# A hybrid encoder layer on one core: side work in the projection phase, first weight loads, dummy matmuls and Newton buffers rearranged

## The chip, the cores and the metric

The kernel runs on one core of a Trainium2 chip. The core has TensorE (PE, matrix products into PSUM), VectorE (DVE), ScalarE (ACT), GpSimd (POOL) and SyncE (SP), and 16 DMA engines that move data between device memory and the on-chip SBUF. Each engine works through its own instruction queue in order, and waits on semaphores for the others. The metric is the device time of one execution in microseconds (us); lower is better.

## The reference

Two inputs, a prompt of 512 tokens and a sample of 2048, go through one encoder layer with shared weights. All 1024-wide matrix products are float32.

```python
def encoder_layer(x, pre_g, post_g, w_in, ...):
    h = rms_norm(x, pre_g)
    z = h @ w_in                       # q k v, gates, u_b, c_val, c_glu, merge gates
    ...
    y_a = neighbourhood_attention(heads(q), heads(k), heads(v), rpb) * jax.nn.silu(gate_a)
    y_b = fourier_mix(u_b) * jax.nn.silu(gate_b)
    y_c = conformer_conv(c_val, c_glu, dw_w, dw_b, cn_g, cn_b) * jax.nn.silu(gate_c)
    merged = (jax.nn.sigmoid(merge_a) * (y_a @ w_a) + jax.nn.sigmoid(merge_b) * (y_b @ w_b)
              + jax.nn.sigmoid(merge_c) * (y_c @ w_c))
    return x + rms_norm(merged @ w_o, post_g)
```

`rms_norm` divides each token's 1024 values by the root of their mean square.

## The kernel before

The 2560 tokens are five chunks of 512: chunk 0 is the prompt, chunks 1 to 4 the sample. Chunks 1 and 2 are projected first, then 3 and 4, then 0. Each float32 operand is split into a high and a low part (`split`: a cast on ACT, L136, and a subtraction on DVE, L137), and every product is three TensorE passes (L180 high x high, L181 high x low, L182 low x high), summed in PSUM.

**Weights** come in units of 512 KB. `emit_unit` loads a unit into a `wraw` tile (three buffers, L144, on SP's queue) and splits it into two half units `w` (five buffers). `unit` keeps up to three units under way. One unit serves one block of 128 outputs for each chunk of the group; a block is 24 matmuls of 128x512.

**Blocks and PSUM.** `mm` gives a block one of three PSUM tiles, so the fourth block waits until the first has been read. In `proj_qk` the order is k for chunk 1, k for chunk 2, q for chunk 1, q for chunk 2, and so on; each result is scaled and moved out of PSUM by DVE at L319 (`z`), split once more (L328 and L329, `zs`) and stored (L331 `qd`, L335 `kds`, four stores each for k).

**Normalisation.** Chunks 1 and 2 start from raw x: `raw_h` makes the tiles `hT` from x transposed (L247, L248), and `raw_scale` works out the factors 1/rms meanwhile (squares at L265, Newton's method on DVE, four small diagonal matmuls at L274, a copy into `rows` on ACT at L275). For chunks 3, 4 and 0 `rstd_rows` does it ahead of time: eight loads `xt` (L209) and squares (L210, ACT) for each chunk, in a tag `xr` of three buffers, then `newton` on a 128x4 tile, then L216 stores the 512 factors to DRAM, in four-byte pieces (`rs`). `make_h` reads that row back, broadcast over the partitions (L223, `rrow`), loads x transposed into the same `xr` buffers (L226) and scales it on DVE (L227).

**Side work.** `newton` takes its tiles `nw_y` and `nw_t` from a tag with two buffers. `dft_parts` copies seven tables of 1 MB from one DRAM place to another (L893, `dftd`), for the Fourier branch, which reads them in the last third of the kernel. Such work is registered with `self.task(generator, steps, start, end)`, and `pump`, called after every few matmuls of the program, takes steps of a task between the positions `start` and `end` (`self.pos` counts the calls; from 60 to 740 us one position takes some 1.4 us). This sets the order in which the program is written; a scheduler that works on a model of the engines then sets the order in each queue, and can put an instruction far ahead of where it was written when nothing that it needs holds it.

**End.** `finish` multiplies by w_o for 128 tokens at a time: two PSUM tiles `po`, for each the sum of squares on ACT (L872, its square written to the SBUF tile `o`) and the product with the post norm's gain on DVE (L873, written to the same half of `o`), then Newton for one value a token, then `ox` at L882 (`o` times the factor plus x) and the store. `o` has one buffer.

Of the kernel before, what the change touches and what calls it, by code (L numbers as in the profile page):

```python
# [15 lines left out]
F32 = mybir.dt.float32  # L16
# [89 lines left out]
class Build:  # L106
# [31 lines left out]

    def emit_unit(self, src, pieces=1):

        raw = self.wraw.tile([P, 1024], F32, tag="wraw", name="wraw")
        n = 1024 // pieces
        for i in range(0, 1024, n):
            self.load = self.nc.sync.dma_start(raw[:, i: i + n], src[:, i: i + n])  # L144
        ws = []
        for i in range(2):
            w = self.wsp.tile([P, 2, 512], F32R, tag="w", name="w")
            self.low = self.split(w, raw[:, i * 512: i * 512 + 512])
            ws.append(w)
        return ws  # L150
# [50 lines left out]
    def rstd_rows(self, c, pool):  # L201

        nc = self.nc
        ss = pool.tile([P, 2, 4], F32, tag="ss8", name="ss8")
        for i in range(4):
            for k in range(2):
                xt = pool.tile([P, C], F32, tag="xr", name="xt", bufs=3)
                row = c * C + i * P
                nc.sync.dma_start(xt, self.a["x"][row: row + P, k * C: k * C + C])  # L209
                nc.scalar.activation(xt, xt, AF.Square, accum_out=ss[:, k, i:i + 1])  # L210
            yield
        v = pool.tile([P, 4], F32, tag="v", name="v")
        nc.vector.tensor_scalar(v, ss[:, 0], 1.0 / D, EPS, op0=ALU.mult, op1=ALU.add)
        nc.vector.scalar_tensor_tensor(v, ss[:, 1], 1.0 / D, v, op0=ALU.mult, op1=ALU.add)
        r = self.newton(pool, "nr", v, nc.vector)
        nc.sync.dma_start(self.rs[c].rearrange("o (t p) -> p (o t)", p=P), r)  # L216
        yield
# [35 lines left out]
    def raw_scale(self, c, pool, rrow):  # L253
# [14 lines left out]
        r = self.rt[c]  # L268
        nc.vector.tensor_copy(r, self.newton(pool, "nr", v, nc.vector))
        ps = self.ps.tile([P, C], F32, tag="s", name="rrow", bufs=2)  # L270
# [584 lines left out]
    def finish(self, c, hh, msp, pool, last):  # L855
        nc = self.nc
        for tt in range(2):
# [5 lines left out]
            for n in range(2):  # L863
                po = self.ps.tile([P, 512], F32, tag="s" if tt == 0 else "pt", name="po", bufs=2)
                for kt in range(KT):
# [5 lines left out]
                    nc.tensor.matmul(po, lhsT=r[:, 1, q], rhs=w[:, 0], start=False, stop=kt == KT - 1)  # L871
                nc.scalar.activation(o[:, n * 512: n * 512 + 512], po, AF.Square, accum_out=ss[:, n:n + 1])  # L872
                nc.vector.tensor_tensor(o[:, n * 512: n * 512 + 512], po, self.postg[:, n * 512: n * 512 + 512], op=ALU.mult)  # L873
# [22 lines left out]
    def run(self):  # L896
        tc, nc, a = self.tc, self.nc, self.a
        with ExitStack() as ctx:
# [25 lines left out]

            self.preg = cst.tile([P, KT], F32, name="preg")
            nc.sync.dma_start(self.preg, a["preg"])
            self.ident = cst.tile([P, P], F32, name="ident")
            make_identity(nc, self.ident)
            self.one = cst.tile([P, P], F32, name="one")
            nc.vector.memset(self.one, 1.0)  # L930


            early = cst.tile([P, 1], F32, name="early")
            nc.scalar.activation(early, self.one[:, 0:1], AF.Tanh)
            ring = F(tc.tile_pool(name="ring", bufs=8, side="left"))
# [26 lines left out]
            def raw(c, ring):  # L962
                yield from self.raw_h(c, hT[c], ring)
                self.raw_scale(c, hp, rows[:, c - 1, :C])
                yield

            first_raw = raw(1, ring2)
            next(first_raw)
            self.ready.append(self.emit_unit(self.queue.pop(0), 2))
            for _ in range(KT - 1):  # L970
# [17 lines left out]
            self.task(seq(self.conv(1, cb[1]), islice(second, 20)), 48, base + 20, base + 340)  # L988
            self.task(self.dft_parts(), 7, base + 30, base + 200)
            self.task(seq(*(self.rstd_rows(c, hp) for c in (3, 4, 0))), 15, base + 20, base + 200)  # L990
            self.proj_qk(hs)
# [164 lines left out]
```

## Time and profile before

| what | value |
|---|---|
| device time, median of 3 runs | 2080.67 us (2077.24 to 2084.29) |
| profiled execution: device time, span in the trace | 2078.99 us, 2077.2 us |
| TensorE busy | 2050.4 us, 99% of the span |
| VectorE, ScalarE, GpSimd busy | 62%, 39%, 15% |
| granted TensorE clock, mean | 0.997 |
| DMA | 388.79 MB, 187 GB/s in the mean |

"Busy" is the share of the span in which an engine executes something. The span is the trace's own length; the device time of the same execution is 1.8 us longer. TensorE's granted clock is a share of full speed (2.4 GHz), 0.5 being 1.2 GHz. In rows of the timeline, "idle before" in brackets is the time for which the engine had stood, and the arrow names what released it.

### The profile page before, as it was taken

How to read it: one execution, taken by the hardware profiler on the slowest of the kernel's cores; microseconds unless marked ns; L12 is line 12 of the kernel's file. 1: busy time of each engine (PE TensorE's matmuls, PEld its weight loads, DVE VectorE, ACT ScalarE, POOL GpSimd, SP SyncE). 2: the span in 40 equal slices, each digit the busy share in tenths (PEclk: the TensorE clock that was granted, in tenths of full speed). 3: DMA queues.
4: the chain of work that ended last, by engine and by line, in shares of the span. 5: the costliest groups of instructions: out<-in, count | busy, mean ns of one | idle time of the engine just before them, and what ended most of it. 6: DMA issues, size and time to landing. Idle time of an engine off the chain costs nothing. (4 is left out here: it accounts for less than half of the span.)

```text
span 2077.2 us, 31264 instructions
## 1 busy us (share of the span) xinstructions
PE 2050.4 (99%) x11184; PEld 1773.8 (85%) x11184; DVE 1296.3 (62%) x2853; ACT 801.3 (39%) x1649; POOL 301.6 (15%) x318
## 2 busy tenths in 40 slices
PE   8899999999999999999999999999999999999998
PEld 6779888888888899888888888898888989999997
DVE  6374557565454546776666655898854666666655
ACT  6422234343332224555555555336654211111111
POOL 0000011111100002322222221003200122222211
PEclk9999999999999999999999999999999999999999
DMA  9694544444443545666566676779897755555532
GB/s 328 202 250 159 181 140 147 142 149 146 142 153 117 152 132 174 178 177 198 172 172 182 177 221 187 239 252 271 267 325 252 225 177 176 185 169 183 178 131 79
DMA packets 241195, 388.79 MB, mean 187 GB/s; under 512 B 25376, under 2 KB 137632, under 8 KB 239136
## 3 DMA queue, kind: packets, MB, share of 16 engines
q1 hardware_dynamic: 241040, 386.80, 60.1%
q8 instruction: 88, 1.44, 0.3%
q14 instruction: 67, 0.55, 0.1%
HBM read 284.47 MB, written 109.58 MB: 190 GB/s over the span
## 5 line engine op out<-in xcount | busy, mean ns | idle before, releaser
L180 PE MATMUL mm<-hT,w 128*128 128x512 f32 x1760 | 699.6, 398 | 15.0 <-ACT w L136 7.1
L181 PE MATMUL mm<-hT,w 128*128 128x512 f32 x1760 | 691.2, 393 | 0.0
L182 PE MATMUL mm<-hT,w 128*128 128x512 f32 x1760 | 690.7, 393 | 0.0
L180 PEld LDWEIGHTS mm<-hT,w 128*128 128x128 f32 x1760 | 332.1, 189 | 79.2 <-ACT w L136 7.3
L182 PEld LDWEIGHTS mm<-hT,w 128*128 128x128 f32 x1760 | 331.7, 188 | 70.3 <-DVE w L137 0.8
L181 PEld LDWEIGHTS mm<-hT,w 128*128 128x128 f32 x1760 | 332.4, 189 | 62.6 <-DVE hT L248 1.0
L137 DVE TENSOR_TENSOR w<-wraw,w 128x512 fp32r<-128x512 f32 x308 | 220.4, 719 | 142.7 <-ACT w L136 138.0
L136 ACT CAST w<-wraw 128x512 fp32r<-128x512 f32 x308 | 189.0, 618 | 201.8 <-PE mm L182 166.2
L459 DVE SCALAR_TENSOR_TENSOR acc<-cb,cw,acc 128x512 f32<-128x512 f32 (+1 forms) x300 | 237.3, 793 | 2.9
L180 PE MATMUL mm<-ysp,wb 128*128 128x256 f32 x640 | 181.7, 284 | 3.8 <-DVE nw_y L118 3.8
L182 PE MATMUL mm<-ysp,wb 128*128 128x256 f32 x640 | 181.7, 284 | 0.0
L181 PE MATMUL mm<-ysp,wb 128*128 128x256 f32 x640 | 181.7, 284 | 0.0
L611 ACT ACTIVATE p<-p,m 128x384 f32<-128x384 f32 (+2 forms) x160 | 102.3, 639 | 153.0 <-DVE m L610 127.8
L607 DVE CUSTOM_DVE_ANT_0 p<-s,bias 128x384 f32<-128x384 f32 (+2 forms) x160 | 92.6, 580 | 104.7 <-PE pt L636 88.1
L574 POOL TENSOR_TENSOR bias<-tab,mask 128x384 f32<-128x384 f32 x64 | 67.4, 1056 | 572.1 <-DVE m L607 529.4
L566 POOL TENSOR_TENSOR bias<-tab,mask 128x512 f32<-128x512 f32 x64 | 85.9, 1344 | 367.5 <-DVE m L607 353.7
L195 PE MATMUL mm<-w,hT 128*128 128x256 f32 x480 | 135.5, 283 | 0.0
L196 PE MATMUL mm<-w,hT 128*128 128x256 f32 x480 | 135.5, 283 | 0.0
L194 PE MATMUL mm<-w,hT 128*128 128x256 f32 x480 | 135.2, 284 | 0.0
L180 PEld LDWEIGHTS mm<-ysp,wb 128*128 128x128 f32 x640 | 123.2, 193 | 5.4 <-DVE th L844 4.0
L870 PE MATMUL po<-wo,msp 128*128 128x512 f32 x320 | 124.5, 390 | 0.0
L869 PE MATMUL po<-wo,msp 128*128 128x512 f32 x320 | 124.3, 391 | 0.1
(154 smaller groups left out, 3000.0 us busy)
## 6 DMA issues: line engine op xcount, KB each, us to landing
wraw<-wn SPq DMA_DIRECT2D x135, 512.0 KB
th<-z SPq DMA_DIRECT2D x120, 256.0 KB
th<-th SPq DMA_DIRECT2D x80, 384.0 KB
qsp<-qd SPq DMA_DIRECT2D x80, 256.0 KB
tab<-tab SPq DMA_DIRECT2D x40, 384.0 KB
w<-dftd SPq DMA_DIRECT2D x14, 1024.0 KB
vsp<-vds SPq DMA_DIRECT2D x256, 48.0 KB
qd<-zs SPq DMA_DIRECT2D x20, 512.0 KB
```

The costliest lines, as they stand in the source:

```text
L136: nc.scalar.copy(dst[:, 0], src)
L137: return nc.vector.tensor_tensor(dst[:, 1], src, dst[:, 0].bitcast(F32), op=ALU.subtract)
L180: nc.tensor.matmul(ps, lhsT=u[:, 0, s], rhs=r[:, 0], start=n == 0, stop=False)
L181: nc.tensor.matmul(ps, lhsT=u[:, 0, s], rhs=r[:, 1], start=False, stop=False)
L182: nc.tensor.matmul(ps, lhsT=u[:, 1, s], rhs=r[:, 0], start=False, stop=n == len(kts) - 1)
L194: nc.tensor.matmul(ps, lhsT=r[:, 0, q], rhs=w[:, 0, s], start=kt == 0, stop=False)
L195: nc.tensor.matmul(ps, lhsT=r[:, 0, q], rhs=w[:, 1, s], start=False, stop=False)
L196: nc.tensor.matmul(ps, lhsT=r[:, 1, q], rhs=w[:, 0, s], start=False, stop=kt == KT - 1)
L459: nc.vector.scalar_tensor_tensor(acc[:, :n], cb[:, b, e:e + n], wv[:, e:e + 1], acc[:, :n], op0=ALU.mult, op1=ALU.add)
L611: nc.scalar.activation(p[:, :n], p[:, :n], AF.Exp, bias=m[:, 1:2], accum_out=m[:, 2:3])
L869: nc.tensor.matmul(po, lhsT=r[:, 0, q], rhs=w[:, 0], start=kt == 0, stop=False)
L870: nc.tensor.matmul(po, lhsT=r[:, 0, q], rhs=w[:, 1], start=False, stop=False)
```

## The change

Five edits, all in the order and the buffers of the work; what is computed stays the same, apart from the 14 matmuls `busy`, whose result is not read.

- The first unit's two half loads go on ACT's queue, ahead of the small Tanh `early`; `preg` is loaded after `ident` and `one` are made in the program. (`unit` keeps using SP's queue for all others.)
- 14 matmuls of 128x128 on the constant `one` stand at the head of TensorE's queue.
- `newton` gets eight buffers instead of two where it works on 128x4 tiles.
- The tasks `dft_parts` and `rstd_rows` are given later positions.
- In `finish` the square is written to a PSUM tile `osq` instead of `o`.

```diff
-    def emit_unit(self, src, pieces=1):
+    def emit_unit(self, src, pieces=1, queue=None):
...
-            self.load = self.nc.sync.dma_start(raw[:, i: i + n], src[:, i: i + n])
+            self.load = (queue or self.nc.sync).dma_start(raw[:, i: i + n], src[:, i: i + n])
...
-        r = self.newton(pool, "nr", v, nc.vector)
+        r = self.newton(pool, "nr", v, nc.vector, bufs=8)
...
-        nc.vector.tensor_copy(r, self.newton(pool, "nr", v, nc.vector))
+        nc.vector.tensor_copy(r, self.newton(pool, "nr", v, nc.vector, bufs=8))
...
-                nc.scalar.activation(o[:, n * 512: n * 512 + 512], po, AF.Square, accum_out=ss[:, n:n + 1])
+                sq = self.ps.tile([P, 512], F32, tag="o", name="osq", bufs=1)
+                nc.scalar.activation(sq, po, AF.Square, accum_out=ss[:, n:n + 1])
...
+            self.ready.append(self.emit_unit(self.queue.pop(0), 2, nc.scalar))
+            early = cst.tile([P, 1], F32, name="early")
+            nc.scalar.activation(early, self.one[:, 0:1], AF.Tanh)
+            busy = self.ps.tile([P, C], F32, tag="o", name="busy", bufs=1)
+            for _ in range(14):
+                nc.tensor.matmul(busy[:, :P], lhsT=self.one, rhs=self.one, start=True, stop=True)
             first_raw = raw(1, ring2)
             next(first_raw)
-            self.ready.append(self.emit_unit(self.queue.pop(0), 2))
...
-            self.task(self.dft_parts(), 7, base + 30, base + 200)
-            self.task(seq(*(self.rstd_rows(c, hp) for c in (3, 4, 0))), 15, base + 20, base + 200)
+            self.task(self.dft_parts(), 7, base + 250, base + 500)
+            self.task(seq(*(self.rstd_rows(c, hp) for c in (3, 4, 0))), 15, base + 140, base + 320)
```

In the changed kernel every line from L873 on is one further down in `finish` (the square is L873, the product L874).

**ScalarE, at the first blocks of chunk 2.** A piece of the difference on ACT's queue (- before, + after); `hT` are tiles of chunk 2, `rows` the factors of chunk 1, `w` the next half units of weights.

```order
-L247 ACTIVATE hT<-xr,preg 128x512 x8
+L247 ACTIVATE hT<-xr,preg 128x512 x6
 L275 COPY rows<-rrow 128x512
-L136 CAST w<-wraw 128x512 x2
+L247 ACTIVATE hT<-xr,preg 128x512 x2
 L395 ACTIVATE z<-z 128x512
-L136 CAST w<-wraw 128x512 x2
+L136 CAST w<-wraw 128x512 x4
```

The copy into `rows` moved two `hT` tiles ahead, and the four casts of weights now stand behind all of `rows`, the two `hT` tiles and `z`, where two of them stood directly behind `rows`.

**SyncE, around the first two stores of factors.** The queue before (the numbers are the scheduler's tile numbers; `rs3` and `rs4` are the factors of chunks 3 and 4):

```order
L209 DMA xt_2361<-x 128x512
L209 DMA xt_2364<-x 128x512
L216 DMA rs3_100<-nw_y_1350 128x4x1
L335 DMA kds_69<-zs_659 64x512 x4
L144 DMA wraw_860<-wn 128x1024
L893 DMA dftd_102<-dft 16x16384
L209 DMA xt_2518<-x 128x512
L335 DMA kds_69<-zs_693 64x512 x4
L216 DMA rs4_101<-nw_y_2206 128x4x1
L209 DMA xt_2521<-x 128x512
L209 DMA xt_2671<-x 128x512
L223 DMA rrow_4413<-rs3_100 128x512
```

The same place in the changed kernel:

```order
L209 DMA xt_4018<-x 128x512
L216 DMA rs3_100<-nw_y_2969 128x4x1
L209 DMA xt_4021<-x 128x512
L209 DMA xt_4190<-x 128x512
L223 DMA rrow_4400<-rs3_100 128x512
L209 DMA xt_4193<-x 128x512
L335 DMA kds_69<-zs_674 64x512 x4
L216 DMA rs4_101<-nw_y_3832 128x4x1
L144 DMA wraw_868<-wn 128x1024
L209 DMA xt_4361<-x 128x512
L209 DMA xt_4364<-x 128x512
L226 DMA xr_4402<-xT 128x512
```

`rs3` is stored one `xt` load earlier; the read back `rrow`, which needs that store to have landed, moved from behind the second store (`rs4`) to ahead of it, ahead of the four `kds` stores too; the first load of `make_h` (`xr_4402`) stands right behind `rs4`, where before it came eight rows after `rrow`; the copy `dftd` is gone from here (seven of them now stand at rows 269 to 422 of SP's queue, 33 to 110 before). The loads and squares `xt` themselves stay where they were.

**VectorE, where PSUM tiles of q and k are read.** Before, from the reading of q for chunk 2 (`z_767`) to the first scaling for chunk 3 (`xr_4415`), with what each waits for:

```order
L319 SCALAR_TENSOR_TENSOR z_767<-mm_741,rows_140 128x512 [waits PE_49]
L137 TENSOR_TENSOR w_774<-wraw_772,w_774 128x512 [waits Activation_49]
L329 TENSOR_TENSOR zs_766<-z_767,zs_766 128x8x4x16 [waits DMAHW2_49,DMAHW1_49,DMAHW3_49,DMAHW0_49,Activation_49]
L319 SCALAR_TENSOR_TENSOR z_806<-mm_780,rows_140 128x512 [waits PE_49]
L213 TENSOR_SCALAR v_3042<-ss8_2360 128x4 [waits Activation_49]
L329 TENSOR_TENSOR zs_805<-z_806,zs_805 128x512 [waits DMAHW1_49,Activation_49]
L214 SCALAR_TENSOR_TENSOR v_3042<-ss8_2360,v_3042 128x4 [waits DVE_49,Activation_49]
L227 SCALAR_TENSOR_TENSOR xr_4415<-xr_4415,preg_103,rrow_4413 128x512 [waits DMAHW7_49]
```

In the changed kernel, from k for chunk 2 (`z_709`) to q for chunk 1 (`z_751`):

```order
L319 SCALAR_TENSOR_TENSOR z_709<-mm_683,rows_138 128x512 [waits PE_49]
L137 TENSOR_TENSOR w_719<-wraw_717,w_719 128x512 [waits DMAHW6_49,Activation_49]
L329 TENSOR_TENSOR zs_708<-z_709,zs_708 128x512 [waits Activation_49]
L227 SCALAR_TENSOR_TENSOR xr_4402<-xr_4402,preg_110,rrow_4400 128x512 [waits DMAHW4_49,DMAHW2_49]
L319 SCALAR_TENSOR_TENSOR z_751<-mm_725,rows_138 128x512 [waits PE_49]
L137 TENSOR_TENSOR hT_4405<-xr_4402,hT_4405 128x512 [waits Activation_49]
L329 TENSOR_TENSOR zs_750<-z_751,zs_750 128x8x4x16 [waits DMAHW6_49,DMAHW7_49,DMAHW5_49,Activation_49]
```

The first scaling of `make_h` (L227), which needs `rrow` and its load, now stands directly ahead of the reading of q for chunk 1; before, it stood behind the reading of the next k. The second Newton's wait for the DMA of `rs3` (in the trace before, the row on DVE at 78.32 us below) is gone from DVE's queue; the same L227 for later tiles stands ahead of `z_782` (q, chunk 2) and, loaded right behind the third store `rs0`, ahead of `z_860` (the next k, chunk 2).

## Rows read from the trace of the kernel before

**Rows 1.** Waits of TensorE, whole span: total us, times, longest.

```profile
PE mm L180 <- ACT w L136: 7.1, 2, 5.9
PE mm L180 <- DVE z L319: 6.6, 2, 4.4
```

**Rows 2.** Stretches: each engine's busy us and instructions, clock, DMA share, GB/s.

```profile
6.00:14.00 8.00, 8.00 (x17) 5.09 (x18) 7.08 (x12) 6.84 (x11) 0.00 (x0) 1.00 1.03 401
14.00:30.00 16.00, 16.00 (x72) 13.20 (x71) 11.26 (x30) 11.83 (x20) 2.25 (x3) 1.00 1.04 398
...
60.00:112.00 52.00, 44.10 (x187) 35.51 (x186) 20.36 (x56) 18.56 (x45) 0.21 (x1) 0.97 0.74 220
...
400.00:740.00 340.00, 340.00 (x1560) 281.82 (x1559) 180.47 (x351) 116.91 (x222) 23.44 (x25) 1.00 0.47 143
740.00:1660.00 920.00, 919.94 (x5058) 793.27 (x5057) 616.16 (x1402) 463.79 (x979) 172.03 (x176) 1.00 0.70 212
```

**Rows 3.** Timeline, all engines, 0 to 7 us: start, duration, engine, work.

```profile
1.65 0.91 SPq L144 DMA_DIRECT2D wraw<-wn  x2
...
4.62 0.72 ACT L247 ACTIVATE hT<-xr,preg 128x512 fp32r<-128x512 f32 x1 [2.40 <-DMA xr<-xT]
5.25 0.60 ACT L136 CAST w<-wraw 128x512 fp32r<-128x512 f32 x1
...
5.91 0.79 PE L180 MATMUL mm<-hT,w 128*128 128x512 f32 x1 [5.91 <-ACT w L136]
```

**Rows 4.** Timeline, 32 to 36 us: chunk 2's first block.

```profile
32.05 1.06 PE L274 MATMUL rrow<-dg,one 128*128 128x128 f32 x8
33.14 0.58 ACT L275 COPY rows<-rrow 128x512 f32<-128x512 f32 x1 [3.21 <-PE rrow L274]
33.62 1.14 ACT L136 CAST w<-wraw 128x512 fp32r<-128x512 f32 x2
...
34.30 0.53 PE L180 MATMUL mm<-hT,w 128*128 128x512 f32 x1 [1.19 <-ACT w L136]
```

**Rows 5.** Timeline of TensorE, 76 to 113 us.

```profile
80.70 0.47 PE L180 MATMUL mm<-hT,w 128*128 128x512 f32 x1 [1.26 <-DVE nw_t L128]
...
96.25 0.77 PE L180 MATMUL mm<-hT,w 128*128 128x512 f32 x1 [4.42 <-DVE z L319]
...
98.95 0.49 PE L180 MATMUL mm<-hT,w 128*128 128x512 f32 x1
...
110.99 0.47 PE L180 MATMUL mm<-hT,w 128*128 128x512 f32 x1 [2.22 <-DVE z L319]
```

**Rows 6.** Timeline of VectorE, 60 to 112 us.

```profile
78.32 0.17 DVE L128 TENSOR_TENSOR nw_t<-nw_y 128x4 f32<-128x4 f32 x1 [7.69 <-DMA rs<-nw_y]
...
106.54 0.76 DVE L227 SCALAR_TENSOR_TENSOR xr<-xr,preg,rrow 128x512 f32<-128x512 f32 x1 [0.20 <-DMA xr<-xT]
```

**Rows 7.** Timeline of SyncE's issues, 55 to 122 us.

```profile
69.34 0.39 SPq L216 DMA_DIRECT2D rs<-nw_y  x1
...
85.05 0.53 SPq L216 DMA_DIRECT2D rs<-nw_y  x1
85.63 7.58 SPq L209 DMA_DIRECT2D xt<-x  x2
```

**Rows 8.** Timeline of ScalarE, 55 to 122 us.

```profile
93.55 0.63 ACT L210 ACTIVATE xt<-xt 128x512 f32<-128x512 f32 x1 [10.25 <-DMA xt<-x]
```

**Rows 9.** DMA throughput, 60 to 125 us, 40 equal slices of 1.6 us.

```profile
GB/s 265 325 281 106 268 216 188 222 59 13 3 1 66 862 0 240 282 121 24 10 28 266 95 368 411 338 397 344 253 400 266 329 397 392 286 136 190 4 33 38
```

**Rows 10.** Timeline, 1663 to 1669 us.

```profile
1665.44 0.60 ACT L872 ACTIVATE o<-po 128x512 f32<-128x512 f32 x1 [8.62 <-DVE ox L882]
...
1666.16 0.69 DVE L873 TENSOR_TENSOR o<-po,postg 128x512 f32<-128x512 f32 x1 [0.81 <-ACT o L872]
...
1668.23 0.38 PE L180 MATMUL mm<-ysp,wb 128*128 128x256 f32 x1 [3.82 <-DVE nw_y L118]
```

**Rows 11.** Costliest groups of the page: the weights' casts.

```profile
L136 ACT CAST w<-wraw 128x512 fp32r<-128x512 f32 x308 | 189.0, 618 | 201.8 <-PE mm L182 166.2
```

More of the change, by code (lines that the diff above doesn't have):

```diff
@@ L923, in run @@
             self.dftd = dram("dftd", [7, P, 2, 1024])
-            self.preg = cst.tile([P, KT], F32, name="preg")
-            nc.sync.dma_start(self.preg, a["preg"])
             self.ident = cst.tile([P, P], F32, name="ident")
@@ L930, in run @@
             nc.vector.memset(self.one, 1.0)
-            early = cst.tile([P, 1], F32, name="early")
-            nc.scalar.activation(early, self.one[:, 0:1], AF.Tanh)
+            self.preg = cst.tile([P, KT], F32, name="preg")
+            nc.sync.dma_start(self.preg, a["preg"])
             ring = F(tc.tile_pool(name="ring", bufs=8, side="left"))
```

## The prediction

> **What bounds the kernel now.** The waits of TensorE come first: the two largest entries are 7.1 us for casts of weights on ACT and 6.6 us for DVE at L319 [rows 1]. Then a table of stretches shows where they lie. From 60 to 112 us TensorE is busy 44.1 of 52 us; from 400 to 1660 us it has no gap worth the name [rows 2]. So the kernel is TensorE's stream of matmuls with a few holes, and only the holes and slow clocks can be won. There are four.
>
> 1. The start: the first matmul is at 5.91 us, released by a cast [rows 3], and the next 8 us hold 17 matmuls where the following 16 us hold 72 [rows 2]: 0.47 us each, then 0.222. The granted clock as a mean reads 1.00 there, but the pace is that of half clock (1.2 GHz).
> 2. At 34 us, 1.19 us before chunk 2's first block, again for a cast [rows 4].
> 3. Between 80 and 111 us three waits of 1.26, 4.42 and 2.22 us, together 7.9, each ahead of a block of q or k that wants its PSUM tile back from DVE [rows 5]. After the longest, the six matmuls from 96.25 to 98.95 us take 0.45 each instead of 0.222: 1.4 us more [rows 5].
> 4. At 1668 us, 3.82 us [rows 10].
>
> The cause of the third is the store of the factors. `rs3` is issued at 69.34 us [rows 7], and DVE stands 7.69 us, to 78.32, because the next Newton wants the tile that this store reads [rows 6]: 9.0 us for 2 KB. Throughput falls to 59, 13, 3 and 1 GB/s in the slices from 73 to 79.5 us, and to 24, 10 and 28 from 89 to 94 us, after the next store at 85.05 [rows 7, 9]. The x load issued right behind that store (85.63) reaches ACT's square at 93.55, 7.9 us on, and ACT had stood 10.25 us for it [rows 7, 8]. Weights' casts lie behind such squares on ACT, readings of PSUM behind casts on DVE, and TensorE behind those.
>
> **The change, part by part.**
>
> *The start.* The first weights' two issues took 0.91 us from 1.65 us on SP [rows 3]; on ACT's queue they go first, about a microsecond sooner. But the first `hT` on ACT began only at 4.62 us, on its x load, and took 0.72 [rows 3], so the first real matmul comes at 5.4 us at best. The 14 dummies: the eight passes of four such matmuls took 1.06 us at full clock [rows 4], 0.13 each, so 28 passes take 3.7 us, twice that at half clock. From about 1 us on they end between 4.8 and 8.5; I take 6, by the start at half clock and a rise on the way. The real work then starts as late as before, but at full pace. Seventeen matmuls at 0.47 become 17 at 0.222 if data kept up: at most 4.2 us. The tiles `hT` still come from ACT one by one, so I take 2.4 by the end of the first block, with 0 and 4.2 as bounds.
>
> The Trainium skill (TensorE: Matmul & The Clock Gate, "Part 1: The HAM clock gate") says that the number of slow matmuls at a start differs from run to run, 6, 11 or 14 of one kernel, and that one shouldn't fit to a count. This trace has about 17 [rows 2], above all of them; with 6 of them the bound would be 1.5 us instead of 4.2.
>
> *At 34 us most of this is lost.* The casts for chunk 2's first block stood directly behind `rows` (33.14 plus 0.58) and TensorE went on at 34.30 [rows 4]. Now two `hT` tiles and a `z` come between. With `rows` 2.4 us earlier it ends at 31.3; two `hT` at 0.72 [rows 3], a `z` priced as a cast, 0.62, and the cast, 0.62 [rows 11], end at 34.0. That is 0.3 us ahead of before; the other casts now come in a row, which saves some of the slow first matmuls behind. I take 0.7 us won in all up to 36 us, between 0 and 2.6 (nothing on ACT in the way).
>
> *Newton's buffers and the later squares, 60 to 112 us.* The order shows that the squares in fact stay early; what changes is who stands behind the stores. DVE's wait of 7.69 us goes: `z_709` (k, chunk 2) is then read in time, and the wait of 1.26 us goes. But the store itself stays as slow, and now SP stands for it, at `rrow`. Step by step: `rs3` one load and the front's gain earlier, about 67.0 us; landed 9.0 later, 76.0; behind `rrow` one x load and four `kds`, six issues of about 0.5 us, put `rs4` at 79.0; `xr_4402`, behind it, lands 8.5 later (85.05 to 93.55 [rows 7, 8]), at 87.5. L227 is 0.76 [rows 6], and `z_751` behind it lets TensorE go about 0.8 after its start: 89.1 us. Two blocks lie between 80.70 and 96.25 us; less the wait of 4.42 that is 5.5 us a block [rows 5]. Without any wait this block (second unit of k, chunk 2) would start at 80.70 - 1.26 - 0.7 + 5.5 = 84.2. So a wait of 4.9 us stands here in place of two, with 1.4 us of slow clock behind it as after the wait of 4.42. The next block starts at 89.1 + 5.5 + 1.4 = 96.0, where before it did at 96.25 [rows 5]. Two blocks later, at 107.0, `z_860` is wanted; its L227 hangs on a load right behind `rs0`. I put that store at 98 us (its Newton needs squares that land with `xr_4402`, and lies between DVE's rows up to `z_821`); plus 8.5 and 1.8 for L227, two small rows and the reading gives 108.3, a wait of 1.3. Before, this block began at 110.99 [rows 5]. **Gain up to here 2.7 us, the front's 0.7 among it.** Bounds: if both loads land in time, the block starts at 84.2 + 3 x 5.5 = 100.7, a gain of 10.3; if `rs0` goes out 5 us later and the slow clock comes too, it starts at 114.7, a loss of 3.7.
>
> *The DFT copies.* Seven times 1 MB leave the stretch 79 to 280 us and come, by their position, at about 400 to 740, where the DMA is 47% busy and TensorE has no gap [rows 2]. The cover is the lead of the weights: their casts stand 166 us in all for TensorE to give buffers back, not for loads [rows 11]. I take 0; without the cover, a copy in front of a weight load costs about 3 us (1 MB at the 400 GB/s of busy slices [rows 9]), once or twice: 0 to 6.
>
> *The last squares.* ACT no longer waits for `ox` (8.62 us [rows 10]) to have a place for its squares. The product on DVE started at 1666.16, 0.81 after `ox`, because of this square; it, the reading of `mm` behind it and TensorE move up by **0.8**. The rest of the 3.82 us is Newton and `ox` ahead of that reading on DVE, and stays. Bounds 0 and 2.3, if a slow clock that follows here too shortens. The very last product still waits for its own square: 0 at the end.
>
> Sum: 2079.0 (the profiled execution) - 2.7 - 0.8 = **2075.5 us**. That execution is 1.7 below the median of the three runs, 2080.67.
>
> **Rivals.**
>
> *The stalls really go.* Loads behind a store are not all held: the store of 69.34 let 59 GB/s through at first [rows 9]. If `xr_4402` lands two or three us after its issue, as loads do elsewhere, `z_751` is in time, and with `rs0` alike the gain is 10.3 + 0.8, more with the front's bound: **2067.9, down to 2065**. For it: DVE's wait of 7.69 us is gone for good, and the copies no longer share the queue here. Against: the load behind the second store took 7.9 us.
>
> *SP's new wait costs more than DVE's old one (slower).* All of SP's queue stands behind `rrow`, and `xr_4402`, `xr_4560` and the load behind `rs0` each hold a reading of PSUM that no such load held before. TensorE follows their landing one for one. After a third store, late in the table of throughput, it is still at 4, 33 and 38 GB/s when the table ends [rows 9], so a load behind a store may take longer than 8.5 us. At 12 us `z_751` is 3.5 later, `rs0` goes out 3.5 later and its load lands 7.0 later; with 1.4 of clock the block of 108.3 starts at 116.7, 5.7 later than before: 2079.0 + 5.7 - 0.8 = **2083.9**. It turns into a loss when the two landings are together about 3.5 us later than counted.
>
> *The change doesn't do what it says.* The squares stay early, the front's gain is eaten at 34 us, the stores' slowness shows elsewhere: 2079 less 0 to 1, **2078.5**.
>
> **How the numbers follow.** The forecast with its waits of 4.9 and 1.3 has 0.42, its own range 2072.5 to 2079; no effect 0.13; the stalls gone, whole or by half, 0.35; the longer landings 0.10. Within 0.3% means 6.2 us, about what a measurement of this kernel can tell from no change; measured from the median that is 2074.4 and below for faster. The stalls gone gives faster nearly always, and a sixth of the forecast's range lies there too: 0.38. Slower by more than 0.3% needs the longer landings whole, or a DFT copy ahead of a weight load that is wanted: 0.08. The rest is 0.54. The range reaches from 2065 (both waits gone, part of the front's bound) to 2081 (forecast with the loss of `rs0`'s bound), and leaves the far end of both outer cases out.
>
> **What would show it.** Right: first real matmul near 6 us at 0.23 us a step; a wait of about 1 us still near 34 us; no wait of DVE on `rs`; SP standing some 9 us at L223; a TensorE wait near 84 to 89 us released by `z` at L319, and a smaller one near 107; the hole near 1664 0.8 us shorter. Wrong: TensorE full from 60 to 112 us (stalls gone), a wait for `w` there (weights late), waits between 400 and 740 us beside L894, or a start where the dummies end after 7 us.

## The result, and the profile after

The changed kernel takes 2098.26 us (median of 6 runs, 2096.31 to 2102.24) against 2077.6 of the kernel before on the same chip (6 runs): ratio 1.0095, interval 1.008 to 1.011. That is slower by 20.7 us, where 3.5 us faster was forecast. The profiled execution took 2102.24 us, the longest of the six; its span is 2100.5.

What TensorE waits for, in the whole span (us in all, times, longest), beside [rows 1]:

```profile
PE mm L180 <- DVE z L319: 17.5, 3, 9.2
PE mm L180 <- DVE nw_y L118: 4.5, 1, 4.5
PE mm L180 <- ACT w L136: 2.9, 1, 2.9
PE busy L972 <- DVE one L929: 1.1, 1, 1.1
```

The start improved: the wait of 5.9 us for the first cast is gone. In its place there are 17.5 us for DVE at L319, in three waits, where before it was 6.6 in two. The same stretches as in [rows 2]:

```profile
14.00:30.00 16.00, 16.00 (x70) 12.91 (x69) 10.68 (x29) 10.53 (x18) 1.88 (x3) 1.00 1.04 396
...
60.00:112.00 52.00, 42.17 (x173) 33.46 (x172) 20.60 (x59) 18.60 (x44) 0.21 (x1) 0.90 0.71 186
112.00:400.00 288.00, 280.33 (x1520) 241.79 (x1519) 169.58 (x325) 87.77 (x168) 17.89 (x16) 0.99 0.47 138
400.00:740.00 340.00, 340.00 (x1553) 279.47 (x1552) 178.56 (x354) 117.90 (x226) 25.32 (x27) 1.00 0.51 164
740.00:1660.00 920.00, 920.00 (x5040) 791.39 (x5039) 611.95 (x1395) 463.02 (x976) 168.20 (x173) 1.00 0.69 210
```

Two things stand out. From 60 to 112 us TensorE is busy 42.17 us instead of 44.10, at a clock of 0.90 instead of 0.97, and now 7.7 us are missing behind 112 us too, where before none were. And from 14 to 30 us, in which it never stands still, it does 70 matmuls where it did 72. The second looks like nothing. It turns out to be some 8 of the 20.7 us (experiments 6 and 12).

**Near 33 us.** ACT's rows, beside [rows 4]:

```profile
31.89 0.59 ACT L275 COPY rows<-rrow 128x512 f32<-128x512 f32 x1 [3.83 <-PE rrow L274]
32.37 1.33 ACT L247 ACTIVATE hT<-xr,preg 128x512 fp32r<-128x512 f32 x2
33.61 0.62 ACT L395 ACTIVATE z<-z 128x512 f32<-128x512 f32 x1
34.12 2.17 ACT L136 CAST w<-wraw 128x512 fp32r<-128x512 f32 x4
```

`rows` is 1.25 us earlier than before (31.89 against 33.14), but the two `hT` and the `z` now delay the first cast to 34.12. TensorE, whose last chunk 1 work ended 1.25 us sooner, waits 2.93 us and goes on at 34.78, half a microsecond later than before. Then it has the half clock (1.2 GHz) for 6 us, which it had not before:

```profile
34.70:41.00 6.30, 6.22 (x14) 4.61 (x15) 4.34 (x10) 6.27 (x13) 0.00 (x0) 0.51 0.61 192
```

At 0.227 each, fourteen matmuls would take 3.2 us, not 6.3. By 41 us the changed kernel is some 3 us behind. How long the half clock lasts behind this wait differs: the six kernels that have this wait of 2.93 us (the changed one and experiments 1, 3, 4, 6 and 11) all have half clock behind it, 6 us in this trace and 3 to 4 us in the other five; those whose wait is 1.19 or 1.20 us have none.

**From 66 to 125 us.** SP's issues, beside [rows 7]:

```profile
66.22 0.39 SPq L216 DMA_DIRECT2D rs<-nw_y  x1
...
75.20 0.33 SPq L223 DMA_DIRECT2D rrow<-rs  x1
...
79.25 0.39 SPq L216 DMA_DIRECT2D rs<-nw_y  x1
...
84.76 0.33 SPq L226 DMA_DIRECT2D xr<-xT  x1
...
109.86 1.14 SPq L216 DMA_DIRECT2D rs<-nw_y  x1
111.05 0.70 SPq L226 DMA_DIRECT2D xr<-xT  x1
```

`rs3` goes out at 66.22 us and `rrow` can be issued at 75.20, 9.0 us later as before. `rs4` goes out at 79.25, and the x load for the first L227 (`xr_4402`) at 84.76: it does not stand right behind `rs4`; a weight load and two x loads lie between, as in the queue listed ahead of the prediction. The third store is at 109.86, its x load right behind. DVE's rows, beside [rows 6]:

```profile
81.78 0.68 DVE L319 SCALAR_TENSOR_TENSOR z<-mm,rows 128x512 f32<-128x512 f32 x1
...
96.28 0.75 DVE L227 SCALAR_TENSOR_TENSOR xr<-xr,preg,rrow 128x512 f32<-128x512 f32 x1 [12.43 <-DMA xr<-xT]
96.95 0.68 DVE L319 SCALAR_TENSOR_TENSOR z<-mm,rows 128x512 f32<-128x512 f32 x1
...
123.02 0.75 DVE L227 SCALAR_TENSOR_TENSOR xr<-xr,preg,rrow 128x512 f32<-128x512 f32 x1 [10.34 <-DMA xr<-xT]
...
124.35 0.68 DVE L319 SCALAR_TENSOR_TENSOR z<-mm,rows 128x512 f32<-128x512 f32 x1
```

L227 waits 12.43 us for the load behind `rs4`: it is there at 96.28, 17.0 us after the store and 11.5 after its own issue. It waits 10.34 us for the one behind the third store, there at 123.02, 13.2 after the store. The reading of PSUM (L319) stands directly or two rows behind, and TensorE behind that, beside [rows 5]:

```profile
97.68 0.79 PE L180 MATMUL mm<-hT,w 128*128 128x512 f32 x1 [9.23 <-DVE z L319]
...
125.18 0.76 PE L180 MATMUL mm<-hT,w 128*128 128x512 f32 x1 [7.67 <-DVE z L319]
```

### The profile page after: what moved, and what is told of

Its sections match the earlier page's. It is cut to its first block, busy times and chain, and to the rows that moved or that the text cites. A ratio compares the mean times of both kernels' runs of the same rounds, so it can differ in the third digit from the quotient of the medians.

```text
span 2100.5 us, 31312 instructions
## 1 busy us (share of the span) xinstructions
PE 2065.9 (98%) x11212; PEld 1781.1 (85%) x11212; DVE 1297.4 (62%) x2853; ACT 803.2 (38%) x1649; POOL 300.8 (14%) x318
## 5 line engine op out<-in xcount | busy, mean ns | idle before, releaser
L180 PE MATMUL mm<-hT,w 128*128 128x512 f32 x1760 | 702.3, 399 | 20.5 <-DVE z L319 17.5
L607 DVE CUSTOM_DVE_ANT_0 p<-s,bias 128x384 f32<-128x384 f32 (+2 forms) x160 | 92.6, 580 | 106.6 <-PE pt L636 89.1
L196 PE MATMUL mm<-w,hT 128*128 128x256 f32 x480 | 134.8, 281 | 0.0
L194 PE MATMUL mm<-w,hT 128*128 128x256 f32 x480 | 134.4, 282 | 0.0
L180 PEld LDWEIGHTS mm<-ysp,wb 128*128 128x128 f32 x640 | 123.8, 193 | 6.1 <-DVE nw_y L118 4.7
L181 PEld LDWEIGHTS mm<-ysp,wb 128*128 128x128 f32 x640 | 123.9, 194 | 1.4
L870 PE MATMUL po<-wo,msp 128*128 128x512 f32 x320 | 124.4, 389 | 0.0
```

The lines of the kernel that those rows point to most:

```text
L180: nc.tensor.matmul(ps, lhsT=u[:, 0, s], rhs=r[:, 0], start=n == 0, stop=False)
L181: nc.tensor.matmul(ps, lhsT=u[:, 0, s], rhs=r[:, 1], start=False, stop=False)
L194: nc.tensor.matmul(ps, lhsT=r[:, 0, q], rhs=w[:, 0, s], start=kt == 0, stop=False)
L196: nc.tensor.matmul(ps, lhsT=r[:, 1, q], rhs=w[:, 0, s], start=False, stop=kt == KT - 1)
L607: nc.vector.tensor_tensor_reduce(out=p[:, :n], in0=s[:, :n], in1=bias[:, :n], scale=1.0, scalar=-3e38, op0=ALU.add, op1=ALU.max, accum_out ...
L870: nc.tensor.matmul(po, lhsT=r[:, 0, q], rhs=w[:, 1], start=False, stop=False)
```

## The experiments

Each experiment is given with its median and the ratio to the kernel before that ran beside it; the median of that kernel was 2080.6 us beside experiments 1 to 4, 2081.8 beside 5 to 8, 2079.8 beside 9 to 12. How a place in memory is named below: `hT` of the pool `ring2` (chunks 1 and 3), `hT` of `ring` (chunks 2, 4 and 0) and the weights `w` each start at some byte of a partition, taken from the built program's memory map; what counts turns out to be the distance between `hT` and `w`.

**1. The first edit alone** (ACT's queue, `preg`, 14 dummies).

```diff
# against the kernel before
+            self.ready.append(self.emit_unit(self.queue.pop(0), 2, nc.scalar))
+            for _ in range(14):
+                nc.tensor.matmul(busy[:, :P], lhsT=self.one, rhs=self.one, start=True, stop=True)
```

> The kernel before with the first edit alone: first weights on ACT's queue, preg later, 14 dummy matmuls. Theory (order): the dummies and the earlier load move the scheduler's model of the start, and this alone puts rrow ahead of the second store of factors, L227 ahead of readings of PSUM, and the two hT tiles ahead of the weights' casts near 33 us. Then most of the loss is here: 2088 to 2098 us, waits of TensorE of 7 us or more between 85 and 126 us, and slow clock after 34 us. Rival (Newton's buffers and later positions do it): the front alone gives 2074 to 2079 us. Rival (the copies of the DFT tables, moved into 300 to 720 us, do it): the same 2074 to 2079.

2085.86 us, ratio 1.0026 (1.0013 to 1.0039): 5.3 us slower. Neither expectation holds whole. The edit alone brings the hole near 33 us with its half clock and a longer wait, but not the two waits behind L227:

```profile
PE mm L180 <- DVE nw_y L119: 8.5, 1, 8.5
PE mm L180 <- DVE z L319: 3.4, 2, 2.7
```

The view names `nw_y`, the row of DVE that ran last before TensorE did; the reading of PSUM that TensorE waits for stands one row ahead of it. The chain leads to a load held behind a store. The second store (`rs4`) goes out at 77.86 us and an x load behind it at 81.51. ACT stands 12.49 us for that load, DVE behind ACT's next cast, and the reading behind DVE:

```profile
94.21 0.63 ACT L210 ACTIVATE xt<-xt 128x512 f32<-128x512 f32 x1 [12.49 <-DMA xt<-x]
94.84 0.60 ACT L328 CAST zs<-z 128x512 fp32r<-128x512 f32 x1
95.47 0.69 DVE L329 TENSOR_TENSOR zs<-z,zs 128x512 fp32r<-128x512 f32 x1 [12.43 <-DMA kds<-zs]
100.04 0.68 DVE L319 SCALAR_TENSOR_TENSOR z<-mm,rows 128x512 f32<-128x512 f32 x1
100.87 0.77 PE L180 MATMUL mm<-hT,w 128*128 128x512 f32 x1 [8.52 <-DVE nw_y L119]
```

This is the path of [rows 8], a square held by a load behind a store, and not Newton's wait for the tile that `rs3` is reading: that one is 5.35 us here, to 73.84, where it was 7.69. The waits behind L227 come only with the change's other edits.

**2. One dummy matmul instead of 14.**

```diff
# against the changed kernel
-            for _ in range(14):
+            for _ in range(1):
```

> The changed kernel with one dummy matmul in place of 14. Theory (order): the queue of ACT near 33 us is that of before again (two casts right behind rows), and rrow stands behind the second store again, so the hole and the slow clock at 34 us go (about 4 us) and the long waits behind L227 shrink: 2078 to 2088 us. Rival (the loss lies in the copies or in the later positions of the squares): 2096 to 2102, the dummies' gain of about 2 lost on top.

2087.66 us, ratio 1.0029 (1.0015 to 1.0043). Within the expectation: the wait for casts is 1.2 us again, and the waits for L319 are 9.0 us in four instead of 17.5 in three. So the wait near 33 us hangs on the dummies. Of the 7.1 us still lost, the place of `ring2` (experiments 5 and 6) can account for all.

**3. Nothing of `make_h` between 60 and 130 us.**

```diff
# against the changed kernel
+        with self.tc.issue_after(self.load.ins):
+            nc.sync.dma_start(rrow, self.rs[c].to_broadcast([P, C]))
...
+            with self.tc.issue_after(self.load.ins):
+                nc.sync.dma_start(xr, self.a["xT"][kt * P: kt * P + P, c * C: c * C + C])
```

> The changed kernel, with rrow and the x loads of make_h tied behind the weight load that is current in the program, so that no L227 stands between 60 and 130 us; squares and the three slow stores stay. Theory (a reading of PSUM stands behind an L227 whose load is held by a store of factors): the waits of 9.2 and 7.7 us with their slow clocks go, some 13 us or more: 2076 to 2087 us. Rival (the stores hold the weights or the squares themselves, L227 only stands beside): 2092 us or more.

2083.96 us, ratio 1.0007 (0.9991 to 1.0022): some 17 us of the 20.7 are back. The waits of TensorE for L319 are 3.2 us in two. The stores themselves stay. The edit takes two things away at once, the L227 ahead of a reading and SP's standing at `rrow`, and does not tell them apart; DVE's rows above show the L227 as the place where the wait arises. In the order of the changed kernel the stores' hold on weights and squares costs at most those 3.2 us; in that of experiment 1 it cost 8.5.

**4. The factors spread by TensorE, no slow store.**

```diff
# against the changed kernel
-        nc.sync.dma_start(self.rs[c].rearrange("o (t p) -> p (o t)", p=P), r)
+        nc.vector.tensor_copy(self.rt[c], self.newton(pool, "nr", v, nc.vector, bufs=8))
...
-        nc.sync.dma_start(rrow, self.rs[c].to_broadcast([P, C]))
+        ps = self.ps.tile([P, C], F32, tag="s", name="rrow", bufs=2)
+        for t in range(4):
+            dg = self.zp.tile([P, C], F32, tag="z", name="dg")
+            nc.vector.tensor_scalar_mul(dg[:, :P], self.ident, self.rt[c][:, t:t + 1])
+            nc.tensor.matmul(ps[:, t * P: t * P + P], lhsT=self.one, rhs=dg[:, :P], start=True, stop=True)
+        nc.scalar.copy(rrow, ps)
```

> The changed kernel without the trip of the factors through DRAM: they stay in SBUF as 128x4, and make_h spreads them with four small diagonal matmuls and a copy on ACT, as chunks 1 and 2 do; no store in four-byte pieces is left. Theory (the slow stores are the root): no wait of TensorE above 2 us from 60 to 130 us; 2070 to 2079 us, the 4 us at 34 us remaining and about 1 us for each of three spreads. Rival (order alone, stores are harmless): no better than with L227 out of the way, 2076 to 2087, or waits of the same size in the same place.

2081.73 us, ratio 1.0005 (0.999 to 1.0021). The waits are gone as expected, and the time is not: above the range. Its stretches:

```profile
14.00:30.00 16.00, 16.00 (x70) 12.85 (x69) 10.42 (x29) 10.30 (x17) 1.99 (x3) 1.00 1.04 396
60.00:112.00 52.00, 52.00 (x228) 42.22 (x227) 28.46 (x72) 20.27 (x46) 0.21 (x1) 1.00 0.75 243
112.00:300.00 188.00, 188.00 (x1105) 166.14 (x1104) 103.49 (x175) 55.24 (x103) 9.86 (x9) 1.00 0.43 133
```

From 60 to 300 us TensorE never stands, where the kernel before loses 7.9 us to waits and 1.4 to clock there, and still the kernel is no faster. So something costs some 8 us that no view of waits shows. The first row has it: 70 matmuls in 16 us, as in the changed kernel, not 72. These 16 us are all chunk 1. In the changed kernel its matmuls start like this:

```profile
25.90 0.40 PE L180 MATMUL mm<-hT,w 128*128 128x512 f32 x1
26.14 0.39 PE L181 MATMUL mm<-hT,w 128*128 128x512 f32 x1
26.37 0.40 PE L182 MATMUL mm<-hT,w 128*128 128x512 f32 x1
26.61 0.39 PE L180 MATMUL mm<-hT,w 128*128 128x512 f32 x1
```

and those of chunk 2 in the same execution:

```profile
45.37 0.39 PE L180 MATMUL mm<-hT,w 128*128 128x512 f32 x1
45.60 0.39 PE L181 MATMUL mm<-hT,w 128*128 128x512 f32 x1
45.83 0.39 PE L182 MATMUL mm<-hT,w 128*128 128x512 f32 x1
46.05 0.39 PE L180 MATMUL mm<-hT,w 128*128 128x512 f32 x1
```

From start to start, as a mean over such blocks, it is 0.233 us against 0.227 (matmuls overlap, and their durations say less than their starts). In the kernel before both chunks have 0.227. What differs between chunks 1 and 2 is the pool of their `hT`. Newton's six more tiles take 32 bytes each, and `ring2` is opened behind their pool: its first tile moves from byte 102,688 to 102,880, while `w` stays at 65,568. The distance goes from 37,120, a multiple of 256, to 37,312, which is 64 less than one.

**5. Newton's eight buffers alone.** All queues have the order of before.

```diff
# against the kernel before, in two places
-self.newton(pool, "nr", v, nc.vector)
+self.newton(pool, "nr", v, nc.vector, bufs=8)
```

> The kernel before with Newton's eight buffers alone; every queue has the order of before. The six more tiles take 32 bytes each, so the ten hT tiles of the pool ring2 (chunks 1 and 3) start 192 bytes further on, at 96 in 128 bytes instead of 32. Theory (address): a matmul of 128x512 that reads such a tile takes 0.233 us instead of 0.227, some 2100 of them: 2084 to 2092 us against 2080.5, less up to 1.3 us for DVE's wait that goes. Rival (the slower pace comes of the moved copies or of the new order): 2077 to 2081 us and 0.227 everywhere.

2086.3 us, ratio 1.0021 (1.0006 to 1.0037): 4.5 us slower (1.3 to 7.7 by the interval). Chunk 1's blocks take 0.233 us from start to start. Summed over the whole trace, against the kernel before, the longer steps come to 8.2 us, in chunks 1 and 3; TensorE's wait of 1.26 us is gone, and some 1.4 us come back where matmuls of another shape are faster (experiment 9). That leaves some 5.5, within the interval.

**6. Ten buffers instead of eight in the changed kernel.** The queues are unchanged; the distance is 37,376, a multiple of 256 as 37,120 is.

```diff
# against the changed kernel, in two places
-self.newton(pool, "nr", v, nc.vector, bufs=8)
+self.newton(pool, "nr", v, nc.vector, bufs=10)
```

> The changed kernel with ten buffers for Newton in place of eight: another 64 bytes, so that hT of ring2 start at 32 in 128 bytes as before the change. Theory (address): blocks of chunk 1 go back to 0.227 us a matmul, 8 to 12 us faster than the changed kernel, 2086 to 2091; the waits near 90 and 120 us stay. Rival (order or copies): 2096 to 2100, pace 0.233 in chunk 1's blocks.

2094.03 us, ratio 1.006 (1.0038 to 1.0081): 12.2 slower than the kernel before beside it instead of 20.7, so some 8 us back, which is in the difference expected (8.5 by the medians, each of which is uncertain by some us; the time itself is above the range, as the kernel before is 4 us higher in this comparison). Chunk 1 is back at 0.227, and the three waits for L319 stay, 16.4 us. So some 8 of the 20.7 us are the place of `ring2` and some 12 the order.

**7. All pools on the left 64 bytes on.**

```diff
# against the kernel before
+            spare = cst.tile([P, 16], F32, name="spare")
+            nc.vector.memset(spare, 0.0)
```

> The kernel before with 64 bytes of an unused constant ahead of the pools on the left: hT of both rings and the weights w all start at 96 in 128 bytes. Theory A (the address of the streamed tile alone counts): all blocks with hT at 0.233, 20 us or more slower, 2100 or more. Theory B (the distance of the streamed tile from the weights that are loaded meanwhile counts, odd multiples of 64 being slow): pace and time as before, 2078 to 2083.

2079.37 us, ratio 0.9995 (0.9981 to 1.0009), 0.227 in both chunks. Theory A falls for this shift: with all moved by 64 bytes, the byte at which a tile starts does nothing by itself.

**8. A candidate: experiment 4 with ten buffers and four dummies.**

```diff
# against the kernel of experiment 4
-            for _ in range(14):
+            for _ in range(4):
...
-self.newton(pool, "nr", v, nc.vector, bufs=8)
+self.newton(pool, "nr", v, nc.vector, bufs=10)
```

> The changed kernel with the factors spread by TensorE as in the fourth run (no store in four-byte pieces), ten buffers for Newton so that all hT and w start at the same place in 128 bytes, and four dummy matmuls in place of 14, with which ACT's queue near 33 us is that of before. Theory (waits behind the slow stores, casts behind hT, and the address, together explain the loss): 2066 to 2073 us. Rival (one of the three is not a cause): 2076 or more.

2073.07 us, ratio 0.9956 (0.9939 to 0.9973): faster than both, by 8.8 us than the kernel before and by some 29 than the changed one (each against the kernel before beside it). The wait for casts near 32 us is 1.2 us again, and the stretch that lost 7.9 us has no gap:

```profile
60.00:112.00 52.00, 52.00 (x231) 43.08 (x230) 31.09 (x81) 21.99 (x51) 0.21 (x1) 1.00 0.84 263
112.00:300.00 188.00, 188.00 (x1109) 167.65 (x1109) 101.94 (x173) 54.68 (x102) 9.85 (x9) 1.00 0.42 132
```

**9. The weights shifted.** 64 unused bytes between `ring` and `w`: now `ring`, which lies ahead of them, is 45,120 bytes from `w` instead of 45,056 (a multiple of 256), and `ring2` moves along with `w`.

```diff
# against the kernel before
+            gap = F(tc.tile_pool(name="gap", bufs=1, side="left"))
+            spare = gap.tile([P, 16], F32, name="spare")
+            nc.vector.memset(spare, 0.0)
             self.wsp = F(tc.tile_pool(name="wsp", bufs=5, side="left"))
```

> The kernel before with 64 unused bytes between the pools of ring and of the weights w: hT of ring (chunks 2, 4, 0) stay at 32 in 128 bytes, w and hT of ring2 (chunks 1, 3) move to 96. Theory (distance from the weights): now the blocks of chunk 2 take 0.233 us a matmul and those of chunk 1 0.227, the other way round from the changed kernel; three chunks are slow instead of two, 2085 to 2093 against some 2081. Rival (a place in memory of its own is bad for ring2's tiles): chunk 1 slow, chunk 2 fast. Rival (neither): all at 0.227 and 2081.

2092.06 us, ratio 1.0064 (1.0046 to 1.0083): 12.2 us slower. Chunk 2's blocks, near 43 us, now have the longer steps:

```profile
43.09 0.39 PE L180 MATMUL mm<-hT,w 128*128 128x512 f32 x1
43.33 0.40 PE L181 MATMUL mm<-hT,w 128*128 128x512 f32 x1
43.56 0.39 PE L182 MATMUL mm<-hT,w 128*128 128x512 f32 x1
43.79 0.40 PE L180 MATMUL mm<-hT,w 128*128 128x512 f32 x1
```

From start to start they take 0.233 us, and those of chunk 1 0.227. Three chunks cost 12.2 us, two some 8 (experiments 6 and 12): some 4 us a chunk on average. The distance from `w` is what counts.

The same distance does the opposite to another shape. Where `hT` is the stationary operand and the weights are streamed (128x256, L194 to L196), TensorE does more of them in 40 us of chunk 0; the first row is the kernel before, the second this one:

```profile
1360.00:1400.00 40.00, 40.00 (x326) 1.00 0.76 261
1370.00:1410.00 40.00, 40.00 (x335) 1.00 0.78 263
```

From start to start these take 0.116 us at best where it was 0.120. In this kernel that gives back some 3.5 us of the 14 that the longer steps cost; the kernels with `ring2` off get back some 1.4.

**10. The copies and the last squares alone.**

```diff
# against the kernel before
-            self.task(self.dft_parts(), 7, base + 30, base + 200)
+            self.task(self.dft_parts(), 7, base + 250, base + 500)
...
-                nc.scalar.activation(o[:, n * 512: n * 512 + 512], po, AF.Square, accum_out=ss[:, n:n + 1])
+                sq = self.ps.tile([P, 512], F32, tag="o", name="osq", bufs=1)
+                nc.scalar.activation(sq, po, AF.Square, accum_out=ss[:, n:n + 1])
```

> The kernel before with two edits alone: the DFT copies at their later positions, and the last squares written to PSUM. Addresses of hT and w as before. By the forecast: 0 and -0.8 us, 2079 to 2081, no wait of TensorE between 130 and 750 us, and the hole near 1664 us down from 4.1 to 3.3. Rival (the copies collide with weights): 2083 or more with waits for w after 300 us. The copies also leave the stretch 60 to 112 us, which may change the waits there by a few us either way.

2078.27 us, ratio 0.9993 (0.9983 to 1.0002), 1.6 below the kernel beside it, which is inside what can be told. No waits between 130 and 750 us. The two edits cost nothing that can be told. (A wait near 1525 us for a table read from `dftd`, of 0.3 to 3.0 us, is in six of the nine traces with the later copies, 1.8 here, and in none of the five without. It was not followed up.)

**11. The candidate with 14 dummies.**

```diff
# against experiment 8
-            for _ in range(4):
+            for _ in range(14):
```

> The candidate of the eighth run with 14 dummy matmuls instead of four; with them the scheduler puts two hT tiles ahead of the weights' casts near 33 us. Theory: the start gains some 2 us, the hole at 31 us grows from 1.5 to 3.2 us and half clock follows it for about 6 us: 1 to 4 us slower than the candidate, 2073 to 2077. Rival (the dummies pay): 1 to 2 us faster than the candidate.

2071.93 us, ratio 0.9963 (0.995 to 0.9976), against 0.9956 of the candidate: no difference that the medians can tell. The traces can: the wait of 2.9 us is there, with half clock behind it for some 3 us (6 were expected), and by 41 us this kernel is 1.9 us behind experiment 8. It stays so up to 1200 us, and the profiled executions differ by 1.5 (2073.19 and 2071.68). That is in line with the loss of 1 to 4 us that was expected, and too little to show in medians of runs that spread over some 9.

**12. The candidate with eight buffers.** Same queues; `ring2` lies 64 bytes off.

```diff
# against experiment 8, in two places
-self.newton(pool, "nr", v, nc.vector, bufs=10)
+self.newton(pool, "nr", v, nc.vector, bufs=8)
```

> The candidate of the eighth run with eight Newton buffers instead of ten, all queues the same: hT of ring2 start 64 bytes in 128 away from w. The clean price of the address, with no wait between 60 and 1200 us in either: chunk 1's blocks at 0.233, 5 to 9 us slower than the candidate, 2077 to 2082.

2079.28 us, ratio 1.0002 (0.9989 to 1.0015), beside 0.9956 of the candidate: -0.5 against -8.8 us, so some 8 us (8.2 by the medians) for the place of `ring2` alone.

## Why the prediction was wrong

The sum: 20.7 us slower = some 8 from the place of `hT` (experiments 6 and 12) and some 12 from the order. Point by point, by the prediction's own steps:

- **Newton's buffers** were priced by the wait that they take away. That was right: no row of DVE waits for the store of `rs` any more (L227 waits once for the read back, 2.2 us). What failed is that nothing was put down for their bytes. Six tiles of 32 bytes shift all that is opened behind them, and with `ring2` 64 bytes off a distance that was a multiple of 256 the 128x512 matmuls of two chunks take 0.233 us instead of 0.227 in blocks with nothing between. Alone this edit makes the kernel 4.5 us slower (experiment 5). No case and no bound of the prediction held this.
- **The squares, 60 to 112 us.** The steps of the chain were right in kind: SP stands at `rrow` until 75.20, 9.0 us after the store (6.2 us of it standing); `rs4` goes out at 79.25 (79.0 counted, and there luck helped: `rs3` went out 0.8 us sooner than counted, and the issues behind `rrow` took 1 us longer); `z_751` stands behind L227, the later block behind the load of the third store. The term that failed is the landing, "`xr_4402`, behind it, lands 8.5 later": it lands 17.0 after the store (96.28 instead of 87.5). It was issued only at 84.76, and then took 11.5. The other is `rs0` "at 98 us", which went out at 109.86, with its load 13.2 behind. TensorE resumed at 97.68 and 125.18 where 89.1 and 108.3 were counted. The block that began at 110.99 in the kernel before begins at 125.18, 14.2 us later, where a gain of 2.7 was counted; the start's loss of some 3 us and the longer steps are among it. In experiment 6, without the longer steps, it begins at 122.12.
- **The rival "SP's new wait costs more than DVE's old one"** is the mechanism that came true; it took 12 us for the landings and ended at 2083.9, with 0.10. With the order alone (experiment 6) the kernel lies 12.2 us over before. Its price was stretched from the one load seen behind a store, 7.9 us. Why the landings are longer is not shown: a weight load and two x loads come between `rs4` and the load that took 17.0, but nothing comes between the third store and the load that took 13.2, and the four stores of k ahead of `rs4` were ahead of it before, too.
- **The start.** The first real matmul is at 6.93 us, not 6 (the dummies end near 7, which the prediction names as a sign of being wrong), but then at 0.23 us a step, and chunk 1's work ends 1.25 us sooner (2.4 counted). "At 34 us most of this is lost" was too mild: the wait is 2.93 us, and half clock follows it until 41 us, which the prediction gave to no wait here. 0.7 us won became about 3 lost. The bounds, 0 to 2.6 won, held no loss. The prediction's own times give the wait: chunk 1's work 2.4 us sooner than 33.1 and the cast's end at 34.0 leave TensorE more than 3 us, not the "about 1 us" that it named as a sign; and it put no slow clock behind it, though it put 1.4 us behind the wait near 84. The Trainium skill (TensorE: Matmul & The Clock Gate, "Part 1: The HAM clock gate") says that one kernel can show 6, 11 or 14 slow matmuls at its start and that one should not fit to a count. Behind the wait here the count differs likewise: 14 in the changed kernel's trace, some 9 in that of experiment 6, with the same queues.
- **The copies** at nothing: nothing that can be told (experiment 10), and no wait for weights beside them. That they cost exactly 0 is not shown: the wait for a `dftd` table near 1525 us comes with them in most traces.
- **The last squares** at 0.8: the mechanism shows. The first product now starts 0.04 us after `ox`, where 0.81 lay between [rows 10]:

```profile
1684.34 0.69 DVE L821 SCALAR_TENSOR_TENSOR yl<-yl,gl 128x512 f32<-128x512 f32 x1 [3.70 <-POOL yl L815]
...
1686.83 1.41 DVE L883 SCALAR_TENSOR_TENSOR ox<-o,nw_y,ox 128x512 f32<-128x512 f32 x2
1688.28 1.29 DVE L874 TENSOR_TENSOR o<-po,postg 128x512 f32<-128x512 f32 x2
```

The hole itself is 4.5 us long all the same, since DVE had stood 3.70 us for POOL's `yl`, which waited for its load. Between kernels with and without the edit it varies from 1.7 to 4.5 us, so 0.8 can't be told in the time.

That two chunks cost some 8 us and not the 12 that 6 ns for all of their 128x512 matmuls would make, the traces show: from 280 to 590 and from 800 to 1290 us, where attention's matmuls run in between, the kernel before already steps at 0.229 to 0.231 us, so less is left to lose there. Experiment 5 has the same 8 us, less what it wins elsewhere.

What stays open: why the distance from the weights counts (only that it does, and not a shift of all by 64 bytes, was shown); what distances other than a multiple of 256 and 64 off one do, 128 off among them, for none was run; why the landings behind a store are so long; and the wait for `dftd`.

## What to carry to other kernels

When TensorE does not stand still and yet a kernel is slower, compare the matmuls' pace, shape by shape and tile by tile, before looking at queues: a few bytes more in one small pool can put the streamed tiles at a distance from the weights at which a matmul takes 2.6% longer (and one that streams the weights past them 1 to 3% less). A store in pieces of four bytes is expensive for whoever queues behind it, not for its own bytes; look at what the scheduler puts there, and if the value fits on chip, spread it on chip. And in a kernel whose order a scheduler decides, every edit at the front is an edit of the whole: the start alone (experiment 1) put `rrow` (73.81 us) ahead of the second store (77.86) in SP's queue, and one dummy matmul instead of 14 (experiment 2) changed the wait near 33 us and those for L319 alike.

## What the runs showed of the hardware

- A 128x512 float32 matmul (one of the three passes), in blocks with no other matmuls between, takes 0.227 us from start to start at the distances between the streamed tile and the weights' tiles that are multiples of 256 bytes (37,120, 37,376 and 45,056), and 0.233 at those 64 bytes off one (37,312 and 45,120); moving all by 64 bytes leaves 0.227 (experiments 5 to 9, 12). No other distances were run.
- A 128x256 matmul that streams the weights past a stationary `hT` goes the other way: 0.120 us from start to start at the first distances, 0.119 at 37,312 (experiment 5) and 0.116 at 45,120 (experiment 9, chunk 0).
- A store of 512 pieces of four bytes took 9.0 us in both kernels, and x loads of 256 KB queued behind one landed 7.9, 13.2 and 17.0 us after it; the first two with nothing between, the third behind a weight load and two x loads.
- A wait of 2.93 us near 32 us was followed by half clock in all six traces that have it, 6 us in one (granted clock 0.51) and 3 to 4 in five; one of 1.19 us at the same place by none.
